# Sliding windows of an image batch: the first loads in other sizes and another order

## Chip, cores, metric

One core of a Trainium2 chip. The metric is the time of one execution on the device in microseconds; smaller is better. Each kernel was run several times and the median is used; one further execution was profiled, and its trace is what is read here.

The engines named below: VectorE (DVE) and ScalarE (ACT) copy between places of the on-chip memory (SBUF), GpSimd (POOL) and SyncE (SP) mainly issue DMAs, as does ScalarE at the beginning. 16 DMA engines move the bytes. TensorE has no work in this kernel.

## Reference

```
x: (16, 64, 64, 64) float32          # batch, channel, height, width
window_size = 8, stride = 4          # n_h = n_w = (64 - 8) // 4 + 1 = 15
result: (16, 15, 15, 64, 8, 8) float32
for i in range(n_h):
    for j in range(n_w):
        result[:, i, j] = x[:, :, 4*i : 4*i + 8, 4*j : 4*j + 8]
```

Nothing is calculated: each 8 x 8 window of each channel is copied out, and since windows overlap by half in both directions, each input value stands in up to four of them. 16.8 MB are read and, by the size of the result, 59.0 MB are written.

## The kernel before

**The input in SBUF.** The tile `L` holds the whole input: 128 partitions, of which 64 (`HP`) belong to each half of the channels (`ch` = 0, 1; `CL` = 32 channels a half). Within a half, a partition is one batch element and one of four bands (`q` in `HQ` = 4) of 16 rows (`RB`); `y` = 0, 1 (`NY`) is the half of the batch, 32 partitions (`QP`) each. Per partition `L` has 32 channels of 16 x 64 values, that is 4 KB a channel, and each channel of a band is one 4 KB packet of a load.

**Two kinds of loads.** The first 8 channels (`FC`) of each half don't go to `L` directly. They are loaded into `S`, two views of the tile `GG` in which the output is put together later, and copied to `L` from there: the staged loads. There are eight (lines 112 to 115): for each band q, one on ScalarE's queue (ch = 0) and one on SyncE's (ch = 1), each 16 partitions x 8 channels, 128 packets, 512 KB. The remaining 24 channels of each half go directly to `L`, 8 partitions a load (lines 117 to 123, through `load`, line 58). For each (y, q), called a turn here, there are a load of ch = 1 with 24 channels on GpSimd, and for ch = 0 either one of 24 channels on GpSimd, or, in the first `HWP` = 6 of the 8 turns, a part of `SMALL` = 4 channels on GpSimd and the other 20 channels on SyncE. So GpSimd issues 16 direct loads and SyncE six.

**The index.** GpSimd writes the partition numbers into `pi` with an iota (line 69), and 20 small VectorE instructions (lines 72 to 101) make of them the tiles `idx`, `idx_y0`, `idx_y1`, `idx_lo` and `idx_hi`: the number of the output row to which each partition's data goes in an indirect store. This part stands ahead of all loads in the program, which for GpSimd means that the iota is issued ahead of its first load; SyncE and ScalarE take no part in it.

**Copies from the staged loads.** 16 copies (line 132) of 32 partitions x 2 channels move `S` to `L`, two of three on VectorE, the third on ScalarE.

**Windows and stores.** `GG` is cut into four buffers (`G`) of 128 partitions x 4096 values, in each of which a row of 16 KB is one output window position with all channels. A unit of work fills one buffer with copies out of `L` (lines 164 to 179, 203) and stores it with one indirect DMA on GpSimd (line 144), 128 rows at most; the buffers are used in turn, so a unit waits for the store of the fourth one before it. `part` (line 195) handles half of the batch, y = 0 first, and is used for the first units, so that these need only the loads of y = 0. The last two stores (line 253), 1 MB each, are plain DMAs on SyncE.

**What sets the order.** Each engine issues its instructions in the program's order; the scheduler adds waits on semaphores. The DMAs of SyncE and ScalarE share eight completion semaphores in turn, those of GpSimd have eight of their own: a DMA that takes a semaphore again waits for the DMA that had it before. So before the change the eight staged loads are issued without a wait, SyncE's six direct loads each wait for one of the first six staged loads, and GpSimd's ninth direct load waits for its first, and so on.

Of the kernel before, what the change touches and what calls it, by code (L numbers as in the profile page):

```python
# [10 lines left out]
def kernel(  # L11
# [7 lines left out]
    nc = tc.nc  # L19
    P = nc.NUM_PARTITIONS  # L20

    B, C, H, W = x.shape
    Bo, NH, NW, Co, WSo, WSo2 = out.shape
    WS = int(window_size)
# [3 lines left out]
    f32 = mybir.dt.float32  # L28
    i32 = mybir.dt.int32
    ALU = mybir.AluOpType  # L30
    CH = 2
    HQ = P // (B * CH)
    CL = C // CH
    RB = H // HQ
# [5 lines left out]
    NY = B // YB  # L40
    QP = YB * HQ
# [4 lines left out]
    gpool = ctx.enter_context(tc.tile_pool(name="gpool", bufs=1))  # L46
# [7 lines left out]
    SMALL, HWP = 4, 6  # L54

    def load(eng, ch, y, q, c0, c1):
        p0 = ch * HP + y * QP + q
        eng.dma_start(out=L[p0 : p0 + QP - HQ + 1 : HQ, c0:c1, :, :], in_=x_v[ch, y, q, :, c0:c1, :])  # L58

    def itile(name):
        return ipool.tile([P, 1], i32, name=name)

    pi, tb, tq, tc_, th, idx, idx_y0, idx_y1, idx_lo, idx_hi = (
        itile(n) for n in ("pi", "tb", "tq", "tc", "th", "idx", "idx_y0", "idx_y1", "idx_lo", "idx_hi")
    )
    FAR = float(2 * B * NWIN)
# [31 lines left out]
    mul(th, tc_, NW)  # L100
    tt(idx_lo, idx_lo, th, ALU.add)


    NG = 4
    GF = C * WS * WS
    GG = gpool.tile([P, NG, GF], f32)
    G = [GG[:, n].rearrange("p (c r w) -> p c r w", c=C, r=WS) for n in range(NG)]
    TC = GF // (RB * W)
    FC = NG * TC // CH
    S = [GG[:, ch * NG // CH : (ch + 1) * NG // CH].rearrange("p n f -> p (n f)").rearrange("p (c r w) -> p c r w", c=FC, r=RB) for ch in range(CH)]  # L110
    x_b = x.rearrange("b (ch cl) (hq r) w -> ch hq b cl (r w)", ch=CH, hq=HQ)
    for q in range(HQ):
        for ch in range(CH):
            s = S[ch][QP + q : QP + q + (B - 1) * HQ + 1 : HQ]
            (nc.scalar, nc.sync)[ch].dma_start(out=s, in_=x_b[ch, q, :, 0:FC, :])

    for y in range(NY):
        for q in range(HQ):
            hw = y * HQ + q < HWP
            if hw:  # L120
                load(nc.sync, 0, y, q, FC + SMALL, CL)
            load(nc.gpsimd, 0, y, q, FC, FC + SMALL if hw else CL)
            load(nc.gpsimd, 1, y, q, FC, CL)

    PC = TC // 2
    first = [(0, ch, c) for ch in range(CH) for c in range(0, FC, PC)]
    then = [(1, ch, c) for ch in range(CH) for c in range(0, FC, PC)]
    for n, (y, ch, c) in enumerate(first + then):
        f = slice(QP + y * QP, QP + (y + 1) * QP)
        d = slice(ch * HP + y * QP, ch * HP + (y + 1) * QP)  # L130
        copy = nc.vector.tensor_copy if n % 3 else nc.scalar.copy
        tc.keep_in_program_order(copy(out=L[d, c : c + PC, :, :], in_=S[ch][f, c : c + PC]))  # L132

# [56 lines left out]
    def tile_():  # L190
        nonlocal at
        at += 1
        return G[(at - 1) % NG]

# [48 lines left out]
    for s in range(2):  # L243
        g = tile_()
        cols = slice(j * ST, j * ST + WS)
        for y in range(NY):
            d = slice(QP + y * QP, QP + (y + 1) * QP)
            for ch in range(CH):
                f = slice(ch * HP + y * QP, ch * HP + (y + 1) * QP)
# [39 lines left out]
```

## Time and profile before

| what | value |
|---|---|
| median of 3 runs | 186.99 us (186.84 to 187.19) |
| the profiled execution | 187.06 us |
| its span, first to last instruction | 185.3 us |
| VectorE busy | 154.2 us (83%) |
| ScalarE busy | 150.7 us (81%) |
| GpSimd busy | 48.3 us (26%) |
| moved by DMA | 75.81 MB, mean 409 GB/s |
| GpSimd's queue (q0) | 8656 packets, 65.55 MB, 84.8% of the engines' time |
| SyncE's queue (q1) | 1744 packets, 8.13 MB, 11.0% |
| ScalarE's queue (q10) | 576 packets, 2.10 MB, 3.1% |

The span is the part of the execution that the trace covers; the remaining 1.8 us lie around it. Times in views of the profile count from the span's beginning. A DMA share is the mean over the 16 DMA engines; packets may overlap on an engine, so that it can exceed 1. Issuing a DMA is not counted as busy time of SyncE and ScalarE. The granted clock was full throughout.

### The profile page before, as it was taken

The numbers are of one execution on the slowest core, as the hardware profiler recorded it, in microseconds if no ns is written. First come the engines' busy times: TensorE is split into PE (matmuls) and PEld (weight loads), VectorE is DVE, ScalarE is ACT, GpSimd is POOL, SyncE is SP. The second block draws the span as 40 slices with busy tenths as digits, with TensorE's granted clock in tenths as the row PEclk, the third lists the DMA queues.
The fourth block names the chain that finished last, engine by engine and source line by source line (L and its number), as shares of the span: only waits on it lengthen the run. The fifth ranks groups of instructions, "written<-read, shape, count | busy, mean of one in ns | idle before, by whom it ended". The sixth has DMA issues, their size and how long they took to land.

```text
span 185.3 us, 597 instructions
## 1 busy us (share of the span) xinstructions
DVE 154.2 (83%) x213; ACT 150.7 (81%) x100; POOL 48.3 (26%) x50
## 2 busy tenths in 40 slices
DVE  5002998999999999799999999999999999999600
ACT  0002999999999999998899999998999999899600
POOL 7400652033308071422222222222222222222000
DMA  4999999999999999999999999999999999999995
GB/s 151 398 410 399 402 402 399 390 382 426 433 424 435 428 428 439 432 430 424 435 430 432 428 432 428 439 417 435 424 423 428 410 435 414 421 428 403 442 414 216
DMA packets 10980, 75.81 MB, mean 409 GB/s; under 512 B 3280, under 2 KB 3280, under 8 KB 7376
## 3 DMA queue, kind: packets, MB, share of 16 engines
q0 software_dynamic: 8656, 65.55, 84.8%
q1 hardware_dynamic: 1744, 8.13, 11.0%
q10 hardware_dynamic: 576, 2.10, 3.1%
q14 instruction: 4, 0.03, 0.0%
HBM read 16.78 MB, written 62.91 MB: 430 GB/s over the span
## 4 chain that ended last, share of the span: by engine, by line
ACT 28%; DVE 28%; DMA 27%; issue 8%; POOL 2%; ACTq 1%; DVEq 0%; PEldq 0%
DVE GG L174 17%; ACT GG L203 17%; DMA L<-in_x_dram 14%; DMA out_dram<-GG,idx 13%; DVE GG L167 11%; ACT GG L164 7%; ACT GG L251 3%; POOL L L58 2%; ACT GG L178 1%; ACTq L284 0%; ACTq L203 0%; POOL pi L69 0%; DVEq L174 0%; PEldq L284 0%; ACTq L164 0%
## 5 line engine op out<-in xcount | busy, mean ns | idle before, releaser
L164 ACT COPY GG<-L 64x2048 f32<-64x2048 f32 x46 | 87.3, 1897 | 5.1 <-DMA out_dram<-GG,idx 2.7
L174 DVE STREAM_SHUFFLE GG<-L 64x1024 f32<-64x1024 f32 (+4 forms) x39 | 53.0, 1359 | 1.3
L167 DVE STREAM_SHUFFLE GG<-L 64x1024 f32<-64x1024 f32 x30 | 38.4, 1281 | 0.0
L203 DVE COPY GG<-L 32x2048 f32<-32x2048 f32 x30 | 36.6, 1219 | 1.8 <-DMA L<-in_x_dram 0.8
L203 ACT COPY GG<-L 32x2048 f32<-32x2048 f32 x18 | 34.1, 1897 | 0.7 <-DMA L<-in_x_dram 0.3
L132 DVE COPY L<-GG 32x2048 f32<-32x2048 f32 x10 | 11.9, 1234 | 13.7 <-DMA GG<-in_x_dram 13.6
L144 POOL DMA_INDIRECT out_dram<-GG,idx_y x6 | 11.0, 1838 | 26.3 <-DVE GG L203 13.2
L58 POOL DMA_DIRECT2D L<-in_x_dram x16 | 12.8, 809 | 19.0 <-DMA L<-in_x_dram 18.5
L144 POOL DMA_INDIRECT out_dram<-GG,idx_lo x8 | 7.7, 961 | 30.8 <-DVE GG L167 23.2
L132 ACT ACT_TABLE_LOAD x1 | 1.3, 1283 | 17.2 <-DMA GG<-in_x_dram 17.2
L144 POOL DMA_INDIRECT out_dram<-GG,idx x8 | 9.7, 1217 | 17.4 <-DVE GG L174 6.8
L144 POOL DMA_INDIRECT out_dram<-GG,idx_hi x7 | 6.7, 961 | 26.6 <-DVE GG L167 22.9
L132 ACT COPY L<-GG 32x2048 f32<-32x2048 f32 x6 | 11.2, 1894 | 0.1
L178 ACT COPY GG<-L 64x256 f32<-64x256 f32 (+2 forms) x21 | 10.2, 484 | 0.5
L164 DVE COPY GG<-L 64x2048 f32<-64x2048 f32 x6 | 7.3, 1222 | 0.2
L251 DVE COPY GG<-L 32x1280 f32<-32x1280 f32 x8 | 6.5, 818 | 0.4 <-DMA out_dram<-GG,idx_hi 0.3
L251 ACT COPY GG<-L 32x768 f32<-32x768 f32 x8 | 6.6, 829 | 0.1
L174 DVE LOAD_MASK_SELECT GG<-L x39 | 0.4, 9 | 1.4 <-ACT GG L164 1.0
L72 DVE TENSOR_SCALAR tb<-pi 128x1 int32<-128x1 int32 x1 | 0.2, 154 | 1.0 <-POOL pi L69 1.0
L179 DVE COPY GG<-L 64x1280 f32<-64x1280 f32 x1 | 0.9, 877 | 0.0
L78 DVE TENSOR_TENSOR th<-tc,tq 128x1 int32<-128x1 int32 x2 | 0.3, 156 | 0.0
L75 DVE TENSOR_SCALAR th<-tc 128x1 int32<-128x1 int32 x2 | 0.3, 154 | 0.0
(21 smaller groups left out, 3.0 us busy)
## 6 DMA issues: line engine op xcount, KB each, us to landing
L<-in_x_dram POOLq DMA_DIRECT2D x10, 768.0 KB, 18.4
L<-in_x_dram SPq DMA_DIRECT2D x6, 640.0 KB
GG<-in_x_dram ACTq DMA_DIRECT2D x4, 512.0 KB, 14.4
GG<-in_x_dram SPq DMA_DIRECT2D x4, 512.0 KB, 14.8
out_dram<-GG SPq DMA_DIRECT2D x2, 1024.0 KB, 10.1
L<-in_x_dram POOLq DMA_DIRECT2D x6, 128.0 KB, 18.2
out_dram<-GG,idx POOLq DMA_INDIRECT x8, 12.4
out_dram<-GG,idx_lo POOLq DMA_INDIRECT x8, 10.3
```

Of the source, the lines that this page charges most:

```text
L58: eng.dma_start(out=L[p0 : p0 + QP - HQ + 1 : HQ, c0:c1, :, :], in_=x_v[ch, y, q, :, c0:c1, :])
L75: nc.vector.tensor_scalar(out=d[:, :], in0=a[:, :], scalar1=float(m), scalar2=None, op0=ALU.mult)
L78: nc.vector.tensor_tensor(out=d[:, :], in0=a[:, :], in1=b[:, :], op=op)
L132: tc.keep_in_program_order(copy(out=L[d, c : c + PC, :, :], in_=S[ch][f, c : c + PC]))
L144: st = nc.gpsimd.indirect_dma_start(out=o_v, out_offset=bass.IndirectOffsetOnAxis(ap=ix[:, 0:1], axis=0), in_=g.rearrange("p c r w -> p (c ...
L164: copy(out=g[d, cs, :, :], in_=L[f, :, s * ST : s * ST + WS, cols])
L167: nc.vector.stream_shuffle(out=g[d, cs, ST:WS, :], in_=L[f, :, 0:ST, cols], mask=nxt)
L174: nc.vector.stream_shuffle(out=out, in_=in_, mask=same)
L178: act(out=out[:, 0:k], in_=in_[:, 0:k])
L179: other(out=out[:, k:], in_=in_[:, k:])
L203: (act if n % 3 == 0 else dve)(out=g[d * QP : (d + 1) * QP, ch * CL : (ch + 1) * CL, :, :], in_=L[f : f + QP, :, s * ST : s * ST + WS, cols],)
L251: copy(out=g[d, ch * CL + c0 : ch * CL + c1, :, :], in_=L[f, c0:c1, s * ST : s * ST + WS, cols])
```

## The change

Three things are changed, all in the loads:

- The first staged load (q = 0) of each of the two queues becomes two: channels 0 and 1 first (32 packets, 128 KB, on ScalarE and then on SyncE), channels 2 to 7 behind (96 packets, 384 KB). The other six staged loads stay.
- The direct loads of the first two turns, (y, q) = (0, 0) and (0, 1), move ahead of the iota and the index arithmetic, the other six turns stay behind it. For GpSimd this puts four loads ahead of the iota.
- Each of SyncE's six direct loads of 20 channels becomes two of 10 channels.

The order of copies, units and stores is as it was. With two more staged loads and six more direct ones, 22 instead of 14 loads take the eight completion semaphores that ScalarE and SyncE share in turn: the two staged loads of q = 3 now wait for the two 2-channel loads, SyncE's first six halves for the other six loads of the stage up to q = 2, the next two halves for the loads of q = 3, and the last four for the first four halves.

```diff
-    nc.gpsimd.iota(pi[:, :], pattern=[[0, 1]], base=0, channel_multiplier=1)
...
     for q in range(HQ):
-        for ch in range(CH):
-            s = S[ch][QP + q : QP + q + (B - 1) * HQ + 1 : HQ]
-            (nc.scalar, nc.sync)[ch].dma_start(out=s, in_=x_b[ch, q, :, 0:FC, :])
-
-    for y in range(NY):
-        for q in range(HQ):
-            hw = y * HQ + q < HWP
-            if hw:
-                load(nc.sync, 0, y, q, FC + SMALL, CL)
-            load(nc.gpsimd, 0, y, q, FC, FC + SMALL if hw else CL)
-            load(nc.gpsimd, 1, y, q, FC, CL)
+        for c0, c1 in ((0, 2), (2, FC)) if q == 0 else ((0, FC),):
+            for ch in range(CH):
+                s = S[ch][QP + q : QP + q + (B - 1) * HQ + 1 : HQ, c0:c1]
+                (nc.scalar, nc.sync)[ch].dma_start(out=s, in_=x_b[ch, q, :, c0:c1, :])
+
+    def direct(y, q):
+        hw = y * HQ + q < HWP
+        if hw:
+            mid = (FC + SMALL + CL) // 2
+            load(nc.sync, 0, y, q, FC + SMALL, mid)
+            load(nc.sync, 0, y, q, mid, CL)
+        load(nc.gpsimd, 0, y, q, FC, FC + SMALL if hw else CL)
+        load(nc.gpsimd, 1, y, q, FC, CL)
+
+    turns = [(y, q) for y in range(NY) for q in range(HQ)]
+    for t in turns[:2]:
+        direct(*t)
...
+    nc.gpsimd.iota(pi[:, :], pattern=[[0, 1]], base=0, channel_multiplier=1)
...
+    for t in turns[2:]:
+        direct(*t)
```

More of the change, by code (lines that the diff above doesn't have):

```diff
@@ L58, in load @@
         eng.dma_start(out=L[p0 : p0 + QP - HQ + 1 : HQ, c0:c1, :, :], in_=x_v[ch, y, q, :, c0:c1, :])
+    NG = 4
+    GF = C * WS * WS
+    GG = gpool.tile([P, NG, GF], f32)
+    G = [GG[:, n].rearrange("p (c r w) -> p c r w", c=C, r=WS) for n in range(NG)]
+    TC = GF // (RB * W)
+    FC = NG * TC // CH
+    S = [GG[:, ch * NG // CH : (ch + 1) * NG // CH].rearrange("p n f -> p (n f)").rearrange("p (c r w) -> p c r w", c=FC, r=RB) for ch in range(CH)]
+    x_b = x.rearrange("b (ch cl) (hq r) w -> ch hq b cl (r w)", ch=CH, hq=HQ)
+    for q in range(HQ):
+        for c0, c1 in ((0, 2), (2, FC)) if q == 0 else ((0, FC),):
[13 more added lines that the diff above has]
+        direct(*t)
     def itile(name):
@@ L101 @@
     tt(idx_lo, idx_lo, th, ALU.add)
[L104 to L111, printed above, removed]
-    for q in range(HQ):
-        for ch in range(CH):
-            s = S[ch][QP + q : QP + q + (B - 1) * HQ + 1 : HQ]
-            (nc.scalar, nc.sync)[ch].dma_start(out=s, in_=x_b[ch, q, :, 0:FC, :])
-    for y in range(NY):
-        for q in range(HQ):
-            hw = y * HQ + q < HWP
-            if hw:
-                load(nc.sync, 0, y, q, FC + SMALL, CL)
-            load(nc.gpsimd, 0, y, q, FC, FC + SMALL if hw else CL)
-            load(nc.gpsimd, 1, y, q, FC, CL)
+    for t in turns[2:]:
+        direct(*t)
     PC = TC // 2
```

## The prediction

> **What bounds the kernel now.** I read the slices of the span first, then a table of stretches, then the chain of waits from its beginning, then the issue times of the loads. The slices (each digit is a share in tenths):
>
> ```profile
> DMA  4999999999999999999999999999999999999995
> GB/s 151 398 410 399 402 402 399 390 382 426 433 424 435 428 428 439 432 430 424 435 430 432 428 432 428 439 417 435 424 423 428 410 435 414 421 428 403 442 414 216
> ```
>
> The DMA engines are full in every slice but the first and the last. The stretches show where they are not (columns: stretch, its length, busy time and count on VectorE, ScalarE and GpSimd, clock, DMA share, GB/s):
>
> ```profile
> 0.00:2.00 2.00, 0.91 (x9) 0.00 (x0) 0.85 (x6) 1.00 0.00 0
> 2.00:2.80 0.80, 0.72 (x7) 0.00 (x0) 0.80 (x2) 1.00 0.61 97
> 2.80:3.40 0.60, 0.50 (x5) 0.00 (x0) 0.60 (x2) 1.00 0.99 307
> 3.40:4.00 0.60, 0.21 (x2) 0.00 (x0) 0.60 (x2) 1.00 0.80 300
> 4.00:5.20 1.20, 0.00 (x0) 0.00 (x0) 1.20 (x3) 1.00 1.08 416
> 5.20:6.00 0.80, 0.00 (x0) 0.00 (x0) 0.80 (x3) 1.00 0.98 323
> 6.00:14.00 8.00, 0.00 (x0) 0.00 (x0) 0.93 (x2) 1.00 1.03 410
> ...
> 45.00:76.00 31.00, 29.26 (x24) 30.61 (x17) 11.42 (x7) 1.00 1.01 432
> 76.00:165.00 89.00, 87.21 (x138) 83.53 (x61) 18.27 (x19) 1.00 1.01 427
> 165.00:174.40 9.40, 8.83 (x10) 9.24 (x10) 1.99 (x2) 1.00 1.00 418
> 174.40:183.00 8.60, 0.00 (x0) 0.00 (x0) 0.00 (x0) 1.00 1.00 427
> ```
>
> From 6 us to 183 us the bytes flow at the rate of their stage. The last copy ends at 174.4 and 8.6 us of stores still drain. So the end is the DMA work plus what is lost before it is full; earlier data moves the end only if the stores behind never run dry. They don't: at 55.70 us, when the fourth store is issued, 16.78 MB of loads and three stores of 2.1 MB (128 rows of 16 KB) had been issued, 23.1 MB, and the stretches add up to 21.4 MB moved (16.8 MB to 45 us, then 10.7 us at 432 GB/s): 1.6 MB, 3.8 us, in hand. At the issue at 165.71 us, 7.3 MB were still to move (8.69 us at 418, 8.6 us at 427) and at most 6.3 MB of that was issued from then on (two GpSimd stores, two SyncE stores of 1 MB): at least 1.0 MB, 2.4 us. I take 2.4 us as the cover of the copies.
>
> What the opening lost, against 410 GB/s: in 2.0 to 2.8, 97 x 0.8 = 78 KB is 0.19 us of work, so 0.61 us are lost; in 2.8 to 3.4, 0.15; in 3.4 to 4.0, 0.16; in 5.2 to 6.0, 0.17. Sum 1.09 us: all that a better opening can save. The chain of waits starts with GpSimd (start, length, what):
>
> ```profile
> 0.84 0.12 POOL pi L69
> 0.96 0.52 issue
> 1.48 4.25 POOL L L58 x7
> 5.74 25.53 DMA L<-in_x_dram
> ```
>
> The iota and 0.52 us in which nothing is issued stand ahead of GpSimd's first load; the first copies out of L wait until 31.27 us. Issue times (ns, min/median/max, then first and last start):
>
> ```profile
> L115 ACTq DMA_DIRECT2D GG<-in_x_dram x4: 613/639/723, 0.7 to 2.7; - x4
> L115 SPq DMA_DIRECT2D GG<-in_x_dram x4: 691/734/814, 0.7 to 3.2; - x4
> L58 POOL DMA_DIRECT2D L<-in_x_dram x15: 551/681/1333, 1.5 to 27.5; - x15
> L58 SPq DMA_DIRECT2D L<-in_x_dram x6: 677/680/3844, 5.1 to 14.2; - x6
> ```
>
> ScalarE and SyncE issue at 0.74, first bytes move after 2.0. By queue, only ScalarE's moves from 2 to 4 us (108 packets), SyncE's joins after 4 us, GpSimd's between 5 and 6 us (6 packets).
>
> **Part 1, the first staged load split into 2 and 6 channels.** Nothing is removed; two DMAs are added (one a queue), bytes unchanged. The climb from 97 to 307 GB/s takes about as long as one issue, 0.64 us: I read it as the 16 DMA engines getting their descriptors one after another, half of 0.64 us late in the mean. If issue time follows the packets, 32 instead of 128 packets take 0.16 us, the mean lateness falls from 0.32 to 0.08: 0.24 us gained, and 0.39 if the 0.15 us of 2.8 to 3.4 goes too. If it is a fixed cost, nothing: SyncE's loads of 160 packets take 680 ns at median against ScalarE's 639 for 128, and the shortest GpSimd issue is 551, so a good part is fixed. Bound below: the 6-channel parts come one issue later, climb as the first load does now, and the 128 KB of ScalarE's first part (0.32 us) may run out before: 0.15 us lost. I take +0.30, nearer the upper bound, because there are now two small first parts on two queues, 256 KB or 0.62 us, to bridge one issue of 0.64 us.
>
> The added DMAs use two more of the eight completion semaphores that SyncE's and ScalarE's DMAs share in turn, so the last staged loads (q = 3) now wait for the two 2-channel parts. Behind ScalarE's there is only its first copy, at 17.2 us, which needs that data anyway; behind SyncE's the direct loads, below. I estimate that those parts land 1 to 2 us after the first bytes, at 3.2 to 4.2 us; today these loads issue at 2.7 and 3.2 and take 14.4 and 14.8 us (median) to land, so up to 1 us later in a full queue costs 0. Without that queue it would cost that 1 us.
>
> **Part 2, the iota behind four GpSimd loads.** GpSimd's first load moves from 1.48 to about 0.8, the 0.12 + 0.52 us go. All eight ungated loads are affected: the first four come 0.6 to 0.7 us earlier, the second four stay, as the iota's 0.64 us now stand there. Bytes do not land earlier where engines are full (4.0 to 5.2, 416 GB/s); but GpSimd's first packets, which come some 4 us behind their issue, would come about 0.7 us earlier, near 5 us, and can fill the hollow of 5.2 to 6.0. With more packets at hand and other sizes of loads the hollow of 3.4 to 4.0 may close too. Bounds 0 and 0.16 + 0.17 = 0.33; a loss is excluded but for rival 3. I take 0.20. The 20 index instructions on VectorE move from 1.0 to about 3.8 us and end near 6.5; VectorE's first copy is at 17.2 and the index is used at 37.09: 0, with 10 us of cover. GpSimd's ninth load waits for its first to land, not for the iota.
>
> **Part 3, SyncE's direct loads in halves.** Six issues become twelve: 6 x 0.68 = 4.1 us on SyncE, which then waits 152.5 us for its stores. With eight semaphores in turn each half waits for an earlier load: the first six for the other staged loads, the next two for the q = 3 ones (now copied from 17.2 on), the last four for the first halves. Today the six are all issued by 18.1 us; the last four halves would go from 17 to about 23 us, as the first halves land. The queue holds about six halves, 6 x 80 packets, when the staged loads are in; at the measured pace of the load stage the y = 0 loads last until 30 us, so the queue stays filled: 0. If it ran dry, each 320 KB would come 0.8 us late on that queue; the copies have 2.4 us of cover.
>
> **Sum.** 0.30 + 0.20 + 0 = 0.5 us. The profiled execution took 187.06 us (span 185.3 and 1.8 around it), which gives 186.56; it lies 0.07 above the median of the runs, 186.99, so I forecast **186.5 us**.
>
> **Rivals.** (1) *Nothing changes*: an issue is a fixed cost, the first 2 channels of the sixteenth engine come as late as 8 did, and the earlier GpSimd packets only share full engines. For it: the nearly equal 639, 680 and 551 ns; against: the climb and the hollows are there. Time 187.0, within 0.3.
>
> (2) *The climb is cured wholly*: both ramps and both hollows go but for 0.2 us: 0.9 gained, 186.1. For it: 256 KB at hand in two queues; against: first packets need their own time, whatever the issue.
>
> (3) *Slower: each added DMA costs a hollow at its seam.* Place: the queues of SyncE and ScalarE; price: that of a hollow, 0.16 us, for each of 8 added DMAs (2 staged parts, 6 halves): 1.3 us, less part 1's 0.3: 188.0. It decides from five seams of eight on (0.8 - 0.3 = 0.5 us lost). For it: 3.4 to 4.0 and 5.2 to 6.0 are where the first loads of two queues are handed over. Against it: from 6 to 14 us the other staged loads are handed over at 410 GB/s without a hollow. The Trainium skill, page "DMA: Bandwidth & Descriptors", section "Rules for kernel authors", speaks for this rival: it wants 1 MiB and more a DMA and many small ones joined, and the section on the anatomy of one DMA gives about 2 us fixed for each, which for eight DMAs in series would be an estimated 16 us. Loads queued behind each other hide it in the row of 6 to 14 us, so by the trace that rule does not bind here.
>
> **How the numbers follow.** The forecast with 0.44, curing wholly 0.12, nothing 0.22, slower 0.22. A measurement of this kernel tells 0.2%, 0.37 us, from no change (the runs lie 0.35 us apart): 186.62 and 187.36 are the bounds. The forecast's own range is 186.3 to 186.7; all of it but 0.04 lies below 186.62, so with rival 2 faster has 0.40 + 0.12 = 0.52, within 0.04 + 0.22 = 0.26, slower 0.22. The range reaches from rival 2 into rival 3: 186.1 to 187.5.
>
> **What would show it.** Right: 2.0 to 2.8 above 200 GB/s and 3.4 to 6.0 near 410 throughout; GpSimd's first load at 0.8 us; the chain's wait for L ending near 30.8 instead of 31.27; the last bytes near 182.5. Part 1 is wrong if the 2-channel issue still takes 0.6 us and the climb is as long; part 2 if GpSimd's first packets come no earlier or 5.2 to 6.0 stays at 323 GB/s; part 3 if the load stage falls below 390 GB/s somewhere between 14 and 45 us. The whole is wrong if the gaps of copies grow past 2.4 us, so that stores run dry.

## The result, and the profile after

The changed kernel is slower: 189.12 us at the median (188.77 to 189.74, 6 runs) against 187.08 us for the kernel before (186.84 to 187.39, 6 runs, measured beside it). The ratio is 1.0115, with a 95% interval of 1.0097 to 1.0132: 2.2 us lost, between 1.8 and 2.5. The profiled execution of the changed kernel took 189.74 us with a span of 188.0, 2.7 us longer than the span before.

The slices of the span of the changed kernel (tenths, then GB/s):

```profile
DMA  4999999999998999999999999999999999999995
GB/s 132 314 408 406 400 398 399 396 387 417 433 432 373 443 425 415 413 432 429 415 420 429 411 443 398 439 415 422 422 417 418 443 394 439 411 425 422 411 432 251
```

By this page nearly nothing has happened: the DMA engines are full again. But the second slice, 4.7 to 9.4 us, moves 314 GB/s where it moved 398, and the thirteenth, near 59 us, has 373 where it had 435. The stretches of the changed kernel (stretch, length, busy time and count on VectorE, ScalarE and GpSimd, clock, DMA share, GB/s):

```profile
2.00:2.80 0.80, 0.00 (x0) 0.00 (x0) 0.80 (x3) 1.00 0.62 148
2.80:3.40 0.60, 0.00 (x0) 0.00 (x0) 0.60 (x3) 1.00 0.97 321
3.40:4.00 0.60, 0.00 (x0) 0.00 (x0) 0.57 (x1) 1.00 0.90 232
4.00:5.20 1.20, 0.90 (x9) 0.00 (x0) 1.16 (x3) 1.00 0.77 246
5.20:6.00 0.80, 0.70 (x8) 0.00 (x0) 0.80 (x3) 1.00 0.80 277
6.00:14.00 8.00, 0.74 (x6) 0.00 (x0) 1.02 (x2) 1.00 1.01 375
14.00:31.00 17.00, 11.52 (x10) 12.47 (x7) 6.90 (x6) 1.00 1.04 401
...
45.00:76.00 31.00, 30.26 (x26) 30.61 (x17) 11.11 (x6) 1.00 1.00 420
76.00:165.00 89.00, 87.52 (x136) 83.76 (x60) 20.25 (x20) 1.00 1.01 422
```

The climb is a little better up to 3.4 us (148 and 321 against 97 and 307 GB/s), and then the rate falls to 232 to 277 GB/s until after 6 us, where it had been 416 in the longest of these stretches. Added up to 31 us, the stretches give 10.8 MB against 11.3 MB before: 0.5 MB, at 410 GB/s 1.2 us behind. That is less than half of the 2.7 us by which this span grew. The rest appears later: 420 against 432 GB/s between 45 and 76 us, and 422 against 427 after.

The first steps of the chain of waits of the changed kernel (start, length, what):

```profile
0.84 0.54 issue
1.38 2.59 POOL L L58 x4
...
4.04 0.16 POOL pi L96
```

The iota now stands behind four loads, but GpSimd's first load starts at 1.38 instead of 1.48 us: the half microsecond in which nothing is issued did not belong to the iota and stayed. Issue times of the staged loads in the changed kernel (ns, min/median/max):

```profile
L74 ACTq DMA_DIRECT2D GG<-in_x_dram x5: 607/622/777, 0.7 to 3.5; - x5
L74 SPq DMA_DIRECT2D GG<-in_x_dram x5: 606/694/850, 0.7 to 3.9; - x5
```

and, in the same columns, of its direct loads:

```profile
L58 POOL DMA_DIRECT2D L<-in_x_dram x15: 548/641/1663, 1.4 to 29.1; - x15
L58 SPq DMA_DIRECT2D L<-in_x_dram x12: 677/677/817, 8.1 to 24.4; - x12
```

The shortest issue on ScalarE is still 607 ns although one of the five now has a quarter of the packets; that one, the first, takes 0.66 us as the whole load did, and on SyncE 0.69 us as before. And SyncE's halves of 80 packets take 677 ns at median, as the whole loads of 160 did (680): an issue is nearly a fixed cost.

The first copies out of `L` and the first store, in the timeline of the kernel before (start, length, engine, line, in brackets the idle time ahead and what ended it):

```profile
30.02 11.50 ACT L203 COPY GG<-L 32x2048 f32<-32x2048 f32 x6 [0.27 <-DMA L<-in_x_dram]
...
37.09 1.76 POOL L144 DMA_INDIRECT out_dram<-GG,idx_y  x1 [4.36 <-DMA L<-in_x_dram]
```

and in the timeline of the changed kernel:

```profile
32.93 9.58 ACT L211 COPY GG<-L 32x2048 f32<-32x2048 f32 x5 [2.29 <-DMA L<-in_x_dram]
...
40.10 1.76 POOL L152 DMA_INDIRECT out_dram<-GG,idx_y  x1 [7.84 <-DMA L<-in_x_dram]
```

The first copy waits 2.3 us for a load and starts 2.9 us later, the first store 3.0 us later. (The 31.27 us of the prediction are the end of the chain's wait for `L`; the first copies out of `L` started at 30.02.) The span grew by 2.7 us. So three things need a cause: the hollow between 3.4 and 8 us, why the first copy is later than the 1.2 us by which the bytes are behind, and why its lateness reaches the end.

### The profile page after: what moved, and what is told of

It reads as the page before. It is cut to its first block, busy times and chain, and to the rows that moved or that the text cites. A ratio compares the mean times of both kernels' runs of the same rounds, so it can differ in the third digit from the quotient of the medians.

```text
span 188.0 us, 608 instructions
## 1 busy us (share of the span) xinstructions
DVE 154.1 (82%) x213; ACT 150.5 (80%) x100; POOL 48.4 (26%) x50
## 4 chain that ended last, share of the span: by engine, by line
DVE 42%; DMA 35%; issue 9%; ACT 5%; POOL 2%; ACTq 0%; DVEq 0%; POOLq 0%; PEldq 0%
DMA L<-in_x_dram 22%; DVE GG L182 18%; DMA out_dram<-GG,idx 13%; DVE GG L211 11%; DVE GG L175 9%; DVE GG L172 3%; ACT GG L259 3%; POOL L L58 2%; ACT GG L172 1%; ACT GG L186 1%; ACTq L292 0%; DVEq L211 0%; POOL pi L96 0%; POOLq L96 0%; DVEq L182 0%
```

## Experiments

All are compared with the kernel before on the same chip, and every median below is to be read against that kernel's, 186.9 to 187.0 us in these comparisons. "The split" is part 1 of the change, "the halves" part 3.

### Each part alone (e1, e2, e3)

```diff
# e1
-        for ch in range(CH):
-            s = S[ch][QP + q : QP + q + (B - 1) * HQ + 1 : HQ]
-            (nc.scalar, nc.sync)[ch].dma_start(out=s, in_=x_b[ch, q, :, 0:FC, :])
+        for c0, c1 in ((0, 2), (2, FC)) if q == 0 else ((0, FC),):
+            for ch in range(CH):
+                s = S[ch][QP + q : QP + q + (B - 1) * HQ + 1 : HQ, c0:c1]
+                (nc.scalar, nc.sync)[ch].dma_start(out=s, in_=x_b[ch, q, :, c0:c1, :])
```

> Part 1 alone: the first staged load of both queues in 2 and 6 channels; iota first, SyncE's direct loads whole. In the changed kernel the rate falls to 246 GB/s in 4.0 to 5.2 us (before: 416), and GpSimd's first packets come before 4 us instead of at 5 to 6. Theory A (the split opens the round of the queues earlier, GpSimd's loads come in early and the opening is hollow): 4.0 to 5.2 below 320 GB/s, GpSimd's packets already before 4 us, at least 1.0 us of the 2.0 us lost: 188.1 or more. Theory B (the moved iota and index arithmetic hollow the opening): 4.0 to 5.2 at 400 GB/s or more, 187.0 +- 0.4. Theory C (the halves deliver the y = 0 loads late): also 187.0 +- 0.4.

Measured: 188.35 us (187.75 to 188.64), ratio 1.006 (1.0043 to 1.0078). The stretches of e1:

```profile
2.00:2.80 0.80, 0.72 (x7) 0.00 (x0) 0.80 (x2) 1.00 0.73 210
2.80:3.40 0.60, 0.50 (x5) 0.00 (x0) 0.60 (x2) 1.00 1.17 307
3.40:4.00 0.60, 0.21 (x2) 0.00 (x0) 0.60 (x2) 1.00 0.73 177
4.00:5.20 1.20, 0.00 (x0) 0.00 (x0) 1.20 (x3) 1.00 0.92 335
5.20:6.00 0.80, 0.00 (x0) 0.00 (x0) 0.80 (x3) 1.00 0.89 246
```

The split alone digs the hollow: 177 GB/s in 3.4 to 4.0 and 246 in 5.2 to 6.0. The stretch from 2 to 8 us as a whole, of the kernel before:

```profile
2.00:8.00 6.00, 1.43 (x11) 0.00 (x0) 4.38 (x8) 1.00 0.95 337
```

and of e1:

```profile
2.00:8.00 6.00, 1.42 (x11) 0.00 (x0) 4.79 (x9) 1.00 0.92 294
```

That is 0.26 MB or 0.6 us of work less. The packets take nearly as much of the engines' time as before (a share of 0.92 against 0.95) for 13% fewer bytes: a packet takes longer on the whole, and engines without packets are not all of the hollow. (Packets may overlap on an engine, so that the share does not exclude idle ones.) Theory A's figure for 4.0 to 5.2 (below 320) is missed by a little, and GpSimd's packets come from 4.0 us on, earlier than 5 us but not before 4.

```diff
# e2: the loads of the first two turns ahead of the iota, all loads as before in size
+    for t in turns[:2]:
+        direct(*t)
...
     nc.gpsimd.iota(pi[:, :], pattern=[[0, 1]], base=0, channel_multiplier=1)
...
+    for t in turns[2:]:
+        direct(*t)
```

> Part 2 alone: four GpSimd loads ahead of the iota, staged and direct loads whole. Theory A: opening as before (4.0 to 5.2 at 400 GB/s or more), GpSimd's packets still only after 5 us, 187.0 +- 0.4. Theory B: 4.0 to 5.2 below 320 GB/s, GpSimd's packets before 4 us, 188.1 or more. Theory C: 187.0 +- 0.4.

Measured: 186.97 us (186.77 to 187.16), ratio 0.9996 (0.9987 to 1.0006). The move of the iota does nothing that can be measured; theory B falls.

```diff
# e3
-                load(nc.sync, 0, y, q, FC + SMALL, CL)
+                mid = (FC + SMALL + CL) // 2
+                load(nc.sync, 0, y, q, FC + SMALL, mid)
+                load(nc.sync, 0, y, q, mid, CL)
```

> Part 3 alone: SyncE's direct loads in halves. Theories A and B: opening and time as before, 187.0 +- 0.4, first copy out of L at 30.0 +- 0.4 us. Theory C: opening as before, first copy out of L at 31.2 us or later (in the changed kernel 32.9), stores begin later than 38.2 us instead of 37.1, and 0.5 to 1.5 us are lost.

Measured: 187.11 us (186.83 to 187.31), ratio 1.0005 (0.9995 to 1.0015), first store at 37.2 us. Six more DMAs of half the size cost nothing by themselves.

### The parts in pairs (e4, e5, e6)

The edits are those of e1 to e3, two at a time.

> Parts 1 and 3, the iota first as before. Theory A: as the changed kernel, 189.1 +- 0.5, 4.0 to 5.2 below 320 GB/s. Theory B: the opening as before, 187.0 +- 0.4. Theory C: opening as before but first copy out of L after 31.2 us, 187.5 to 188.5.

Measured: 189.26 us (188.81 to 189.36), ratio 1.0112 (1.0095 to 1.0129), as the changed kernel. Its hollow lies between those of e1 and of the changed kernel (205 GB/s in 3.4 to 4.0, 270 in 4.0 to 5.2, 246 in 5.2 to 6.0).

> Parts 1 and 2, SyncE's direct loads whole. Theory A: 188.1 or more, the opening hollow (4.0 to 5.2 below 320 GB/s); if the opening is all of it, 189.1 +- 0.5. Theory B: the same. Theory C: 0.5 to 1.5 us faster than the changed kernel: 187.6 to 188.6, first copy out of L at 31.5 us or earlier instead of 32.9.

Measured: 188.31 us (188.04 to 188.78), ratio 1.0075 (1.0055 to 1.0095), the first copy out of `L` at 31.1 us. The time is in the range of theory A and of theory C, the copy is where theory C had it.

> Parts 2 and 3, the staged loads whole. Theory A: opening as before, 187.0 +- 0.4. Theory B: hollow opening, 188.1 or more. Theory C: opening as before, first copy out of L after 31.2 us, 187.5 to 188.5.

Measured: 187.07 us (186.95 to 187.35), ratio 1.0005 (0.9995 to 1.0015).

What follows from the six: no kernel without the split is slower than before, every kernel with it is. The halves cost 0 without the split (e3, e6) and 0.9 us beside it (189.26 against 188.35 on the same chip). So theory A is right that the split is what costs; whether it costs by GpSimd's early loads, as the theory put it, is tried in e10. Theory C, as it was put, falls: the halves are late only when the opening is.

### What of the split it is: its size, its number, GpSimd (e7, e8, e10, e11)

```diff
# e7                                  # e11: (0, 4), (4, FC)
-        for c0, c1 in ((0, 2), (2, FC)) if q == 0 else ((0, FC),):
+        for c0, c1 in ((0, 6), (6, FC)) if q == 0 else ((0, FC),):
```

> Only the first staged load split, but into 6 and 2 channels. Theory D (cover: the engines live on the first load of each queue until the next loads' packets are at hand; 2 + 2 channels are 64 packets, 0.64 us, and run dry at 3.2 us, 8 + 8 are 2.6 us): 6 + 6 are 192 packets, 1.9 us, so most of the loss is gone: 187.4 or less, 4.0 to 5.2 at 390 GB/s or more. Theory F (each added DMA costs, by its seam or because the q = 3 loads now wait for a semaphore): as with 2 and 6, 188.3 +- 0.4. Theory E (GpSimd's loads come into the round early, and that hollows the opening): in between, since GpSimd's turn comes after 192 instead of 64 packets, near 5 us: 187.3 to 187.9.

Measured: 187.64 us (187.16 to 188.12), ratio 1.0037 (1.0025 to 1.0049). By the ratios that is 0.7 us, against 1.1 for 2 and 6 channels: theory F, in which every split costs the same, is off by 0.7 us; theory D had the loss smaller than it is (its 4.0 to 5.2 us came, 396 GB/s, its time did not); theory E's range holds the time.

```diff
# e8
-        for c0, c1 in ((0, 2), (2, FC)) if q == 0 else ((0, FC),):
+        for c0, c1 in ((0, 2), (2, FC)) if q == HQ - 1 else ((0, FC),):
```

> The last staged load (q = 3) instead of the first is split into 2 and 6 channels; as many DMAs and semaphore waits as in the split of q = 0, the opening as before. Theories D and E: 187.0 +- 0.4, 4.0 to 5.2 at 400 GB/s or more. Theory F: 188.3 +- 0.4.

Measured: 187.19 us (187.01 to 187.36), ratio 1.0014 (1.0005 to 1.0024): 0.3 us. As many DMAs and as many waits on semaphores as in e1, but the opening is untouched (420 GB/s in 4.0 to 5.2): the number is not it. Nor is it that loads go later by their waits for semaphores: SyncE's first direct load is issued at 7.82 us in e1 instead of 5.07, but in e8 at 9.16; its last staged load goes at 3.70 us in e1 instead of 3.16, but in e7, which loses less, at 5.44.

```diff
# e10: the split of e1, and ahead of GpSimd's loads
+    late = ipool.tile([P, 512], f32, name="late")
+    for _ in range(8):
+        tc.keep_in_program_order(nc.gpsimd.memset(late[:, :], 0.0))
```

> The split into 2 and 6 channels with GpSimd's loads held back by eight fills of a scratch tile, so that its packets come after 6 us as nothing can be early. Theory E: 4.0 to 6.0 at 380 GB/s or more, 187.5 or less. Theory D: 3.4 to 4.0 still below 220 GB/s, 4.0 to 5.2 below 380, 188.3 +- 0.5.

GpSimd's loads are kept in program order besides, so that they stay behind the fills. Measured: 189.12 us (188.5 to 189.25), ratio 1.0106 (1.0086 to 1.0126). The queues between 4 and 6 us in e10 (packets, MB, share of the 16 engines):

```profile
q1 hardware_dynamic: 69, 0.26, 53.6%
q10 hardware_dynamic: 70, 0.23, 34.0%
```

and its stretches:

```profile
3.40:4.00 0.60, 0.20 (x2) 0.00 (x0) 0.54 (x2) 1.00 1.02 246
4.00:5.20 1.20, 0.00 (x0) 0.00 (x0) 1.08 (x3) 1.00 0.79 246
5.20:6.00 0.80, 0.00 (x0) 0.00 (x0) 0.80 (x2) 1.00 1.01 241
```

GpSimd's queue (q0) does not appear at all, and the hollow is as deep as in the changed kernel. Theory E falls: SyncE's and ScalarE's queues make it between themselves. (3.4 to 4.0 has 246, not below 220 as theory D had it.) Here too the packets take long: the shares of 1.02 and 1.01 in the first and the last stretch go with 246 and 241 GB/s, where before, from 6 to 14 us, 1.03 went with 410. The kernel is slower than e1; GpSimd's first load is issued at 5.45 us instead of 1.48, and the first store comes at 38.96 us instead of 38.51.

> Only the first staged load split, into 4 and 4 channels: the first two loads together have 128 packets, 1.3 us of work. Theory D (the loss goes with what the first loads lack of 256 packets): between the splits into 2 and 6 (188.35) and 6 and 2 (187.64): 187.7 to 188.3. Theory F (any split of the first load costs the same): 188.35 or 187.64, as one of the two.

Measured: 187.80 us (187.22 to 188.32), ratio 1.0038 (1.002 to 1.0056). Inside theory D's range and within 0.2 us of the split into 6 and 2, so that F's reading is not excluded by this run: what the three splits show is that the small first part of 2 channels costs more than one of 4 or 6, not a clean line.

### Which of the two loads, and whether it must be the first (e13, e14, e15)

```diff
# e13: ScalarE's first load split, SyncE's whole     # e14: the other way round
+                if q == 0 and ch != 0:
+                    if c0:
+                        continue
+                    lo, hi = 0, FC
+                else:
+                    lo, hi = c0, c1
```

> Only ScalarE's first staged load is split into 2 and 6 channels; SyncE's stays whole, so the first two loads hold 32 + 128 = 160 packets. Theory D (the packets of the first two loads together decide): a loss as for 128 to 192 packets, 0.7 us: 187.3 to 188.0. Theory I (the load that is first in line decides, and that is ScalarE's): the whole loss of the split, 188.1 or more. Theory J (any split in the opening costs by its number): half of the loss, 187.5 +- 0.3.

Measured: 187.78 us (187.65 to 188.79), ratio 1.0062 (1.0038 to 1.0086).

> Only SyncE's first staged load is split into 2 and 6 channels; ScalarE's stays whole: 128 + 32 = 160 packets. Theory D: as ScalarE's alone, 187.3 to 188.0. Theory I: no loss, 187.0 +- 0.3. Theory J: 187.5 +- 0.3.

Measured: 187.22 us (187.09 to 188.65), ratio 1.0028 (1.001 to 1.0047).

```diff
# e15
-        for c0, c1 in ((0, 2), (2, FC)) if q == 0 else ((0, FC),):
+        for c0, c1 in ((0, 2), (2, FC)) if q == 1 else ((0, FC),):
```

> The second staged load of both queues (q = 1) is split into 2 and 6 channels, the first stays whole: the first two loads hold 256 packets. Theories D and I: 187.0 +- 0.4, 4.0 to 5.2 at 400 GB/s or more. Theory J: as the split of q = 0, 188.1 or more.

Measured: 187.31 us (187.18 to 187.44), ratio 1.0021 (1.0011 to 1.003), 396 GB/s in 4.0 to 5.2.

By these profiles the deep hollow needs both first loads split: with one of them whole there are 386 (e13) and 399 GB/s (e14) in 4.0 to 5.2. By the medians, splitting the load that is first in line costs 0.8 us, the second 0.3, the third and fourth 0.4. By the ratios it is 1.2, 0.5 and 0.4, the first as much as both together (1.1), and the intervals of e13 and e14 overlap. So theory J falls with e15, while theories D and I are not told apart: I asked for 188.1 or more in e13, and the median is 187.78 but the ratio gives 188.1; D had e14 a little too high. What stands is that every split in the opening costs, and that nothing shows one that gains. Why e13 to e15 cost anything with little hollow to see is taken up under e9.

### How lateness reaches the end (e9)

```diff
# e9: the kernel before, in part()
+            for _ in range(2 if (y, j) == (0, 0) and n < 3 else 1):
                 tc.keep_in_program_order(
                     (act if n % 3 == 0 else dve)(
```

> The kernel before with the first three copies out of L made twice (one more on ScalarE, 1.9 us, two more on VectorE, 2.4 us), so that all later copies are some 1.9 us later and no load or store is changed. Output the same. If the stores have 2.4 us of cover, as the prediction took: 187.4 or less. If the copies are the bound from there on and the end follows the first store one to one: first store at 39.0 +- 0.3 us instead of 37.1, time 188.5 to 189.1.

Measured: 189.11 us (189.03 to 189.29), ratio 1.012 (1.0103 to 1.0137); first store at 39.37 us, 2.3 us later than before, and 2.2 us lost, a little beyond what was expected if the copies are the bound. No load was touched, and the opening is as before. One stretch of e9:

```profile
59.00:62.00 3.00, 2.94 (x3) 2.98 (x2) 2.35 (x2) 1.00 0.74 311
```

The same stretch of the kernel before:

```profile
59.00:62.00 3.00, 2.94 (x3) 2.98 (x2) 1.06 (x1) 1.00 1.01 431
```

of e1:

```profile
59.00:62.00 3.00, 2.94 (x3) 2.98 (x2) 1.85 (x1) 1.00 1.01 431
```

and of the changed kernel:

```profile
59.00:62.00 3.00, 2.91 (x4) 2.95 (x3) 2.35 (x2) 1.00 0.90 382
```

Near 59 us the DMA engines run out of stores in e9, as its half-microsecond stretches show:

```profile
59.00:59.50 0.50, 0.50 (x1) 0.50 (x1) 0.50 (x1) 1.00 0.54 229
59.50:60.00 0.50, 0.47 (x2) 0.50 (x1) 0.34 (x1) 1.00 0.08 33
60.00:60.50 0.50, 0.50 (x1) 0.50 (x1) 0.01 (x1) 1.00 0.93 393
```

The rate recovers at 60.0 us, 2.0 us after the fourth store was issued at 57.98. Before, that store is issued at 55.70 and the engines stay full. So the cover at that place was about 1.4 us (57.7, when its bytes begin, to 59.1), and lateness beyond it is lost there: 0.8 us in e9 (311 against 431 GB/s for 3 us). The rest of e9's loss comes at the stores behind it. The changed kernel, whose loads are 1.2 us behind and whose first store is 3.0 us late, has the same hole (382 GB/s). In e1 the first store is 1.4 us late (38.51) and the loads are 0.7 us behind (16.53 MB against 16.82 moved by 45 us), so that the stores do not run dry at 59 us. But e1 loses another 0.6 us between 76 and 165 us:

```profile
76.00:165.00 89.00, 86.37 (x137) 83.80 (x59) 18.89 (x20) 1.00 1.01 424
```

where the kernel before has 427 GB/s. Over the whole run next to nothing of a late start is covered. In the profiled executions, by how much the first store comes later than 37.09 us, and by how much the span is longer than 185.3 us:

| run | first store later, us | span longer, us |
|---|---|---|
| e15 | 0.3 | 0.4 |
| e13 | 0.6 | 0.6 |
| e7 | 0.6 | 0.7 |
| e11 | 0.7 | 0.6 |
| e5 | 1.3 | 1.2 |
| e1 | 1.4 | 1.6 |
| e12 | 1.5 | 1.3 |
| e10 | 1.9 | 2.2 |
| e9 | 2.3 | 2.0 |
| e4 | 2.6 | 2.2 |
| changed kernel | 3.0 | 2.7 |

In e2, e3, e6, e8 and e14 neither is above 0.3; what the medians of e8 and e14 lose, 0.3 us each, their profiles do not explain. The end follows the first store nearly one to one, whether loads or copies made it late. e9 shows it with the loads untouched. e13 agrees: it has moved as many bytes as the kernel before by 45 us (16.86 against 16.82 MB), but its first store comes at 37.65 us,

```profile
37.65 1.76 POOL L151 DMA_INDIRECT out_dram<-GG,idx_y  x1 [4.36 <-DMA L<-in_x_dram]
```

and its span is longer all the same. So what a change of the loads costs here is read from the first store and not from the bytes moved in the opening. Why the first copies come later than the bytes are behind (1.4 against 0.7 us in e1, 0.6 against none in e13) stays open; which load they wait for was not tried by itself.

### Where the halves cost (e12)

```diff
# e12: the split, and halves for y = 1 alone
+                mid = (FC + SMALL + CL) // 2 if y else CL
+                load(nc.sync, 0, y, q, FC + SMALL, mid)
+                if y:
+                    load(nc.sync, 0, y, q, mid, CL)
```

> The split into 2 and 6 channels and halves for SyncE's last two direct loads alone (y = 1); its four loads for y = 0 stay whole. Theory G (what the halves add, 0.9 us beside the split, comes from the y = 0 loads, which take the semaphores in turn and so wait longer for their issue): first copy out of L at 31.5 +- 0.3 us and 188.35 +- 0.4, as with the split alone. Rival H (the halves cost by their number or by the rate of the load stage, wherever they stand): about a third of the 0.9 us or more stays: 188.6 to 189.3.

Measured: 188.08 us (187.6 to 188.53), ratio 1.0058 (1.0035 to 1.0081), as the split alone. The first copy out of `L` in the timeline of e1:

```profile
31.46 9.58 ACT L204 COPY GG<-L 32x2048 f32<-32x2048 f32 x5 [1.67 <-DMA L<-in_x_dram]
```

of e4:

```profile
32.49 9.58 ACT L206 COPY GG<-L 32x2048 f32<-32x2048 f32 x5 [2.28 <-DMA L<-in_x_dram]
```

and of e12:

```profile
31.50 9.58 ACT L207 COPY GG<-L 32x2048 f32<-32x2048 f32 x5 [2.17 <-DMA L<-in_x_dram]
```

With halves for y = 0 the first copy is 1.0 us later, with halves for y = 1 alone it is not. Theory G holds as to the place: the 0.9 us come with the y = 0 halves. That it is the semaphores taken in turn that hold them back was not tried by itself; in e3 the y = 0 halves wait on semaphores too, and cost nothing. Some of it may not be the halves' own: from 2 to 8 us, with at most one half issued (e4, at 7.46 us), the profile of e4 has 270 GB/s, that of e1 294 and that of e12 321, though all three begin with the same loads. One profile of an opening is therefore good to about 0.4 us of work.

## Why the prediction was wrong

The forecast was 186.5 us, and slower had a chance of 0.22; measured was 189.12, above the range. Step by step:

- *Part 1, +0.30 us taken, bounds -0.15 to +0.39.* This is the step that failed. e1 shows a loss of 1.1 us by its ratio (0.8 to 1.5), outside the bounds. The prediction did see what could go wrong, the first parts running out before the next load's packets arrive, but priced it as one climb of 0.15 us, done by 3.4 us. In e1 the hollow begins at 3.4 us, and by 8 us 0.6 us of work are missing, four times that price; the rest of the loss comes later, by the late copies (see the cover, below). By queue, the trace of e1 has 37 packets of ScalarE and nearly none of SyncE from 3.2 to 4.0 us (7, of no size), after both had moved together from 2.4 to 3.2. Before, ScalarE's first load alone fed the engines to 4 us, and SyncE's then followed with 102 of 138 packets from 4.0 to 5.2, at 416 GB/s. I read it as the engines taking one queue's load after the other, the first loads being what covers the arrival of the next. This reading is not shown, and it is not all of the cause: from 2 to 8 us the packets of e1 take 0.92 of the engines' time, against 0.95 before, for 13% fewer bytes, so that they take longer. Why they do stays open. Shown is that the split costs (e1 against e2 and e3), and that it is the small part at the head of the queues (e7, e8, e11).
- *"Nearer the upper bound, because there are now two small first parts on two queues."* That choice was the wrong one, and the rows were there to say so: 639 ns for 128 packets, 680 for 160, 551 for 32 on GpSimd. The issue is a fixed cost, as rival 1 had it; the changed kernel has 607 at the least.
- *Part 2, +0.20 us taken, bounds 0 to 0.33.* e2: 0, the lower bound. GpSimd's first load came 0.1 us earlier, not 0.7. The iota was charged with 0.52 us of issue that belong to GpSimd's first load. Where its packets do come early, in the changed kernel before 4 us (41 packets), they are not what digs the hollow: e10 has it as deep without them.
- *Part 3, 0.* Right alone (e3), wrong beside the split: 0.9 us, by the y = 0 halves (e12).
- *The cover of 2.4 us.* Wrong, and this is why the loss was not limited to the opening. The bytes issued but not moved were counted at the moment of the issue; a store's first bytes come 2.0 us after it (e9). So the 3.8 us in hand at 55.70 us were about 1.4 (e9), and the 2.4 us at 165.71 us are an estimated 0.4. e9 lost 2.2 of its 2.3 us. I looked for what the copies could hide and took the full DMA engines for the only bound; the copies were a second one, almost as tight. The profile before had said so: on the chain that ended last ScalarE and VectorE have as much as the DMAs each,

```profile
ACT 28%; DVE 28%; DMA 27%; issue 8%; POOL 2%; ACTq 1%; DVEq 0%; PEldq 0%
```

- *Rival 3* had the sign and about half of the loss (188.0), but the wrong mechanism: it charged each added DMA with a hollow at its seam. Six added halves cost nothing (e3), two added staged parts later in the queue 0.3 us (e8), two at the head 1.1 us (e1). The rule of the Trainium skill that stood beside it, page "DMA: Bandwidth & Descriptors", section "Rules for kernel authors" (large DMAs, small ones joined), pointed the right way at the head of the queue (1.1 us, e1); in e3, behind full queues, nothing of it was to be seen. (The 2 us for each DMA that the prediction took from that page of the Trainium skill are given there for the DMAs of GpSimd's path, and the added ones are SyncE's and ScalarE's.)

The terms of the real sum: the split 1.1 us, the halves beside it 0.9, the iota 0: 2.0, against the 2.2 us (1.8 to 2.5) that the change cost. None of the kernels tried is faster than the one before.

## What to carry to other kernels

Do not split the first loads of a queue to get the first byte of work sooner unless the issue time is seen to fall with the size: here it did not, and a small first part on two queues cost 1.1 us. When counting how much work a queue has in hand, count from the first byte of the next transfer, not from its issue. And a full DMA row in the slices does not say that the engines feeding it have room: delay them by a known amount and look whether the end moves, as e9 does.

## What the runs showed of the hardware that was not expected

- The issue of a load on ScalarE or SyncE takes 0.55 to 0.69 us at the least, in no order of size: the first one 0.66 and 0.69 us with 32 packets (e1) as with 128 (before), a later one of 128 packets 0.55 us (e7), those of 80 (e3) and 160 packets (before) 0.68 us. On GpSimd it is 0.55 us.
- In the opening, with 128-packet loads waiting on two queues, only ScalarE's packets move until about 4.0 us; with 32-packet first parts, both queues move (0.13 MB each from 2.4 to 3.2 us, e1), and GpSimd's first packets come between 4.0 and 4.4 us (e1) or before 4 us (changed kernel) instead of after 5 us, though the issue moved by at most 0.1 us.
- In e10 the rate stays at 241 to 246 GB/s from 3.4 to 6.0 us, with loads issued from 0.74 us on and packets taking 0.79 to 1.02 of the engines' time.
- An indirect store of 128 rows of 16 KB takes GpSimd 1.86 us to issue, and its first bytes come 2.0 us after the beginning of the issue (e9).
